# Squared norms of q in a hybrid S5 / gated-DeltaNet layer: turns of 32x32 squares, sums and a regrouping through DRAM in place of products with a column of ones

## The chip, the core and the metric

The kernel runs on one core of a Trainium2 chip. The metric is the device time of one execution in microseconds (us). The engines are PE (TensorE matmuls), PEld (TensorE weight loads, which overlap PE), DVE (VectorE), ACT (ScalarE), POOL (GpSimd) and SP (SyncE, which issues nearly all transfers here).

## What is computed

One residual layer on x of 1024 x 2048 in float32: a norm, one wide input projection, an S5 state-space branch, a gated DeltaNet branch of 8 heads x 128, a merge and an output projection. The change lies in the DeltaNet branch, where q and k of each head are divided by their lengths:

```python
def l2norm(t):
    return t * lax.rsqrt(jnp.sum(t * t, axis=-1, keepdims=True) + EPS)
...
q = l2norm(q.reshape(bsz, l, DN_HEADS, DN_HEAD_DIM))
k = l2norm(k.reshape(bsz, l, DN_HEADS, DN_HEAD_DIM))
...
o = gated_delta_rule(q, k, v, g, beta)
o = rmsnorm(o, norm_w) * jax.nn.silu(z)
```

Because o is linear in q and is normed itself afterwards, the kernel never divides q: the sum of squares of each q row goes into the small term of o's norm, at the end of the head.

## The kernel before

The sequence is worked in two passes of 512 tokens. In each pass PE goes through a plan of projection columns in stripes of 128 (`plan`): for each head its k, q, v and z stripes and two gate stripes, with the S5 input stripes `u` in between, then the S5 gate stripes, then the up projections and the output projection. A stripe is a sum over 16 (or 8) k-tiles, and each k-tile is three products of 128 x 128 by 128 x 512, since each operand is split into a high part and a low rest (`whi`, `wlo`). The weights come in halves of 512 KB (`raw`, three buffers, loaded on SP's queue); ACT copies a quarter-stripe chunk of them to `whi`, DVE subtracts to get `wlo`, and `w_next` keeps four chunks (`LA = 4`, four k-tiles each) ready ahead of PE.

All other work is written as Python generators in lanes (`epi`, `io`, `chain`, `prep`, `tab`, `s5`, `out`, `x`). After each k-tile `pump()` lets each lane take one step, if a planner (`Clock`, fed by the table `COST`) thinks that the step's inputs are there and that DVE is not too far behind PE. The planner's times only set the order in which instructions are written; each engine then works through its own list in that order, and waits where an input is not ready. `drain` writes out all that is left of a lane.

The lane `prep` holds `d_prep(h)`, one per head: ACT squares q into the tile `LU` (128 features x 512 tokens), PE turns k (`ident` products into bank 2), ACT squares the turned k with running sums, DVE writes `kd` (the row `M<-p,ex`), PE multiplies `LU` with a column of ones (bank 5, read by DVE into `nq_`), then k times k and k times q (`p<-M`, 128 x 256), a triangular solve with a trip through DRAM (`lu_d`, `tu_d`), all on slices of one tile block that the profile calls M. `d_chain(h)` follows with the state recurrence, and reads `nq_` at its end. Small per-token vectors lie in one tile, `smalls`.

The lane `s5` holds `s5_gen`: PE products into banks 6 and 7 (`p<-G0b`), then for two pairs a run of DVE work in the tile G0a (products with `p`, sums, two scans, products, and the sums into `sx`), then the output products `p<-G0a,G0b` of four `sx` pieces. In the first pass `s5_setup` runs ahead of it; its last stage is a loop of twelve 128 x 1024 DVE operations on the tile Y, and all that is left of it is drained when the plan comes to the first `u` stripe.

Where q's epilogue ends (`conv_epi`), DVE writes q into M by a SCALAR_TENSOR_TENSOR (`M<-tmp`), and all of the above for that head comes after it.

Of the kernel before, what the change touches and what calls it, by code (L numbers as in the profile page):

```python
# [11 lines left out]
F32 = mybir.dt.float32  # L12
# [4 lines left out]
AX = mybir.AxisListType  # L17
# [19 lines left out]
P = 128  # L37
# [56 lines left out]
class Timed:  # L94
# [3 lines left out]
    def __getattr__(self, name):  # L98
# [41 lines left out]
_VG = {"V": (0.07, 1.04e-3), "G": (0.14, 2.1e-3), "S": (0.05, 0.9e-3)}  # L140
_VF = {"V": (0.1, 0.6e-3), "G": (0.12, 1.1e-3), "S": (0.05, 0.9e-3)}
COST = {"tensor_tensor": _VG, "scalar_tensor_tensor": _VG, "tensor_scalar": _VF, "tensor_copy": _VF,
        "tensor_reduce": _VG, "activation": _VG, "tensor_tensor_scan": {"V": (0.07, 1.28e-3)},
        "memset": _VF, "reciprocal": {"V": (0.07, 8.3e-3)}, "iota": _VG, "matmul": None, "transpose": None, "dma_start": None}


@with_exitstack
def kernel(
# [27 lines left out]
    V = Timed(nc.vector, "V", clock)  # L176
    S = Timed(nc.scalar, "S", clock)
    G = Timed(nc.gpsimd, "G", clock)
    PE = Timed(nc.tensor, "PE", clock)
    SP = Timed(nc.sync, "Q", clock)  # L180
# [8 lines left out]
    dram = ctx.enter_context(tc.tile_pool(name="dram", bufs=1, space=bass.MemoryType.DRAM))  # L189
# [4 lines left out]
    def nm(s):  # L194
        uid[0] += 1
        return f"{s}_{uid[0]}"

    def bank(i):
        return psum.tile([P, 512], F32, tag=f"p{i}", name=nm(f"p{i}"))
# [7 lines left out]
    def small(tag, n, rows=P):  # L207
        if tag not in small_at:
            small_at[tag] = small_at.get("", 0)
            small_at[""] = small_at[tag] + n  # L210
        return smalls[0:rows, small_at[tag]:small_at[tag] + n]

    def tt(o, a, b, op, eng=None):
        (eng or V).tensor_tensor(o, a, b, op=op)

    def ts(o, a, s1, s2, op0, op1=None):
        if op1 is None:
            V.tensor_scalar(o, a, s1, None, op0=op0)
        else:
            V.tensor_scalar(o, a, s1, s2, op0=op0, op1=op1)  # L220
# [4 lines left out]
    MUL, ADD, SUB, MAX, MIN = ALU.mult, ALU.add, ALU.subtract, ALU.max, ALU.min  # L225
# [4 lines left out]
    ones = cpool.tile([P, P], F32, name="ones")  # L230
# [45 lines left out]

    lu_d = [dram.tile([4, 129, P], F32, name=f"lu_d{i}") for i in range(2)]
    tu_d = [[dram.tile([4, 129, P], F32, name=f"tu_d{i}{j}") for j in range(2)] for i in range(2)]
    st_d = dram.tile([8, P, P], F32, name="st_d")
    td_d = dram.tile([16, P, T], F32, name="td_d")  # L280
    ts_d = dram.tile([16, P, T], F32, name="ts_d")

    def part(d, off, *dims):

        a = d[:, :, :] if len(d.shape) == 3 else d[:, :, :, :]
        return bass.AP(tensor=a.tensor, offset=a.offset + off, ap=[list(x) for x in dims])
# [5 lines left out]
    def rows(d):  # L292
        return d[:, 0:P, :].rearrange("c s n -> s c n")
# [42 lines left out]
    def gts(o, a, s1, s2, op0, op1):  # L336
        G.tensor_scalar(o, a, s1, s2, op0=op0, op1=op1)
# [10 lines left out]
    for ps_ in range(NPASS):  # L348
# [8 lines left out]
        for c in range(8):  # L357
            if c % 2 == 0 and 8 - u0 + c // 2 < 8:
                i = 8 - u0 + c // 2
# [718 lines left out]
    def bc4(a):  # L1078
        return a.unsqueeze(2).broadcast_to([P, 4, P])
# [10 lines left out]
    def d_prep(h, ps_):  # L1090
        st = dw["set"][h % 2]
        kq, v, qk, U, kd = st["kq"], st["v"], st["qk"], st["U"], st["kd"]
        E, LU, mi = dw["E"], dw["LU"], dw["mi"]
        nk_, nq_, cc_ = nk[h % 2], nq[h % 2], cc[h % 2]
        lud, tud = lu_d[h % 2], tu_d[h % 2]
        pD = bank(5)
        for j in range(2):
            for i, gg in enumerate((gth, gtl)):
# [4 lines left out]
                          start=(i == 0), stop=(i == 1))  # L1103
# [9 lines left out]
            S.activation(mi[:, c, :], pK[:, c * P:(c + 1) * P], AF.Square, accum_out=nk_[:, c:c + 1])  # L1113
        tt(kd, pK.rearrange("p (c n) -> p c n", c=4), bc4(ex[:, 1, h * 4:(h + 1) * 4]), MUL)
        yield
        pQ = bank(5)
        for c in range(4):
            PE.matmul(pQ[:, c:c + 1], lhsT=LU[:, c, :], rhs=ones[:, 0:1], start=True, stop=True)

        rk = small("rk", 4)  # L1120
        gts(nk_, nk_, 1.0, 4e-6, MUL, ADD)
# [1 line left out]
        tt(cc_, cc_, bt[:, h, :], MUL, eng=G)  # L1123
        pow_small(rk, nk_, 4, "half")
        gts(rk, rk, 0.5, 1.0, MUL, MUL)
        ts(nq_, pQ[:, 0:4], 128e-6, 512e-12, MUL, ADD)
        yield
        for hf in range(2):
            pA = bank((5, 2)[hf])
            for c in (2 * hf, 2 * hf + 1):  # L1130
                PE.matmul(pA[:, (c % 2) * 256:(c % 2) * 256 + 256], lhsT=kq[:, c, 0, :],
                          rhs=kq[:, c].rearrange("p a n -> p (a n)"), start=True, stop=True)
# [2 lines left out]
            tt(qk[:, 2 * hf:2 * hf + 2, :], pa[:, :, 1, :], E[:, 2 * hf:2 * hf + 2, :], MUL)  # L1135
            yield
        tt(LU, LU, bc4(cc_), MUL)
        yield
        SP.dma_start(rows(lud), LU)
        yield  # L1140
# [11 lines left out]
        for j in range(15):  # L1152
            n = 15 - j
            a = ba[:, j, j + 1:16].unsqueeze(2).broadcast_to([32, n, j + 1])
            b = btm[:, j:j + 1, 0:j + 1].broadcast_to([32, n, j + 1])
# [33 lines left out]
        for b in B4:  # L1189
            for c in range(4):  # L1190
                PE.matmul(pU[b, c * 32:(c + 1) * 32], lhsT=g3[b, c, :], rhs=U[b, c, b], start=True, stop=True)
                PE.matmul(pU[b, P + c * 32:P + (c + 1) * 32], lhsT=U[b, c, b], rhs=g3[b, c, :],
                          start=True, stop=True)
# [8 lines left out]
        for o in (0, 64):  # L1202
            for c in range(4):
                PE.matmul(pg[o + 32:o + 64, c, 0:32], lhsT=LU[o:o + 32, c, o + 32:o + 64],
                          rhs=Tm[o:o + 32, c, o:o + 32], start=True, stop=True)
# [5 lines left out]
        for o in (0, 64):  # L1211
            for c in range(4):
                PE.matmul(pu[o:o + 32, c, 0:32], lhsT=gs[o + 32:o + 64, c, 0:32],
                          rhs=U[o + 32:o + 64, c, o + 32:o + 64], start=True, stop=True)
                PE.matmul(pu[o + 32:o + 64, c, 0:32], lhsT=U[o + 32:o + 64, c, o + 32:o + 64],
                          rhs=gs[o + 32:o + 64, c, 0:32], start=True, stop=True)
        for o in (0, 64):
            S.activation(U[o:o + 32, :, o + 32:o + 64], pu[o:o + 32, :, 0:32], AF.Copy, scale=-1.0)
        for o in (0, 64):
            S.activation(Tm[o + 32:o + 64, :, o:o + 32], pu[o + 32:o + 64, :, 0:32], AF.Copy, scale=-1.0)  # L1220
        yield

        pG = bank(5)
        pg = pG.rearrange("p (c n) -> p c n", c=4)
        for c in range(4):
            PE.matmul(pg[64:128, c, 0:64], lhsT=LU[0:64, c, 64:128], rhs=Tm[0:64, c, 0:64],
                      start=True, stop=True)
# [4 lines left out]
        for c in range(4):  # L1232
            PE.matmul(pu[0:64, c, 0:64], lhsT=gs[64:128, c, 0:64], rhs=U[64:128, c, 64:128],
                      start=True, stop=True)
# [140 lines left out]
    for ps_ in range(NPASS):  # L1375
# [49 lines left out]
        for kind, i, c0 in plan[ps_]:  # L1425
# [128 lines left out]
            elif kind in "qkv":  # L1554
                if kind == "k":
                    add("prep", i, d_prep(i, ps_))
# [126 lines left out]
```

## Time and profile before

| | |
|---|---|
| device time, median of three runs | 3029.99 us (3028.96 to 3030.83) |
| profiled execution, its own time | 3029.73 us |
| its span, first to last instruction | 3027.8 us |
| PE busy | 2974.2 us (98%) |
| DVE busy | 1662.4 us (55%) |
| ACT busy | 1152.2 us (38%) |
| mean granted TensorE clock | 0.993 of full speed |

All lines of the kernel pass through one recording helper, so every row has the line number L135, and groups are told apart by the names of their tiles, with buffer numbers left out. A float32 product is recorded as two matmuls with two weight loads. Time between the span and the device time (1.9 us) lies before the first and behind the last instruction.

### The profile page before, as it was taken

The page shows a single profiled execution, that of the slowest core. Times are in us where ns is not written, and L with a number is a line of the kernel's source. Part 1 is how long each engine was busy: PE and PEld are TensorE (multiplying, and loading weights), DVE is VectorE, ACT ScalarE, POOL GpSimd, SP SyncE. Part 2 cuts the span into 40 slices and gives each one's busy share as a digit, 9 for nine tenths or more (in the row PEclk, how much of TensorE's full clock was granted, in tenths as well). Part 3 has the DMA queues.
Part 4 walks back from the last instruction along what each step waited for, and adds up shares of the span by engine and source line. Part 5 has one row for each costly group of instructions (what it writes and reads, how often), then busy time and mean ns, then how long its engine had stood idle before and what let it go on. Part 6 is the DMA issues. An engine that isn't in the chain of part 4 may idle for free.

```text
span 3027.8 us, 42544 instructions
## 1 busy us (share of the span) xinstructions
PE 2974.2 (98%) x16030; PEld 2391.6 (79%) x16030; DVE 1662.4 (55%) x3082; ACT 1152.2 (38%) x2483; POOL 449.3 (15%) x857
## 2 busy tenths in 40 slices
PE   8989999999999999999999999999999999999998
PEld 6877777777777888888878777777777788888887
DVE  5746676777777522553454575567557633226542
ACT  5434544554454222334333333333433322223331
POOL 4412222122200000000033221222112000000000
PEclk9999999999999999999999999999999999999999
DMA  6525444444445644446354344444444464445541
GB/s 168 133 57 154 122 121 130 111 117 122 133 135 166 191 122 120 144 134 238 119 160 134 108 114 115 133 114 117 119 126 120 123 207 122 122 122 153 197 151 56
DMA packets 582143, 405.02 MB, mean 134 GB/s; under 512 B 55161, under 2 KB 515122, under 8 KB 580018
## 3 DMA queue, kind: packets, MB, share of 16 engines
q1 hardware_dynamic: 579634, 393.92, 45.3%
q0 software_dynamic: 2304, 8.39, 0.8%
q8 instruction: 126, 2.06, 0.3%
q14 instruction: 79, 0.65, 0.1%
HBM read 335.66 MB, written 66.58 MB: 133 GB/s over the span
## 4 chain that ended last, share of the span: by engine, by line
PE 85%; DVE 7%; POOL 2%; ACT 2%; issue 1%; DMA 1%; SPq 0%; DVEq 0%; POOLq 0%; ACTq 0%
PE p L135 85%; DVE G0a L135 2%; POOL M L135 2%; DVE M L135 2%; DVE wlo L135 1%; DVE tmp L135 1%; ACT M L135 1%; DMA raw<-in_w_in_dram 0%; DVE Y L135 0%; POOL smalls L135 0%; DMA M<-tu_d 0%; SPq L135 0%; ACT whi L135 0%; ACT L135 0%; ACT tmp L135 0%
## 5 line engine op out<-in xcount | busy, mean ns | idle before, releaser
L135 PE MATMUL p<-X,whi 128*128 128x512 f32 (+1 forms) x4432 | 1398.7, 398 | 1.9 <-DVE whi L135 0.8
L135 DVE TENSOR_TENSOR wlo<-raw,whi 128x512 fp32r<-128x512 f32 x920 | 631.0, 698 | 700.9 <-ACT whi L135 700.1
L135 PEld LDWEIGHTS p<-X,whi 128*128 128x128 f32 (+1 forms) x4432 | 802.8, 188 | 177.1 <-issue 19.9
L135 PE MATMUL p<-X,wlo 128*128 128x512 f32 (+1 forms) x2184 | 854.2, 391 | 8.0 <-DVE wlo L135 7.9
L135 ACT ACTIVATE whi<-raw 128x512 fp32r<-128x512 f32 x917 | 557.7, 625 | 512.6 <-PE p L135 485.0
L135 PE MATMUL p<-Y,whi 128*128 128x512 f32 (+1 forms) x1808 | 568.8, 396 | 1.9 <-ACT whi L135 1.1
L135 PEld LDWEIGHTS p<-X,wlo 128*128 128x128 f32 x2184 | 411.7, 189 | 97.6 <-DVE wlo L135 9.1
L135 PEld LDWEIGHTS p<-Y,whi 128*128 128x128 f32 (+1 forms) x1808 | 329.9, 187 | 72.8 <-ACT whi L135 2.6
L135 PE MATMUL p<-Y,wlo 128*128 128x512 f32 x896 | 349.8, 390 | 0.0
L135 POOL TENSOR_SCALAR smalls<-smalls 128x4 f32<-128x4 f32 (+1 forms) x58 | 15.7, 270 | 1603.8 <-DVE smalls L135 1109.4
L135 ACT ACTIVATE tmp<-p 128x512 f32<-128x512 f32 x160 | 95.5, 597 | 401.8 <-PE p L135 391.9
L135 POOL TENSOR_TENSOR M<-M 32x28 f32<-32x28 f32 (+8 forms) x492 | 190.7, 388 | 289.4 <-DMA M<-lu_d 194.2
L135 DVE TENSOR_TENSOR G0a<-G0a 128x256 f32<-128x256 f32 (+1 forms) x432 | 212.3, 528 | 3.4
L135 PEld LDWEIGHTS p<-M 32*32 32x32 f32 (+2 forms) x3072 | 153.5, 123 | 72.6 <-ACT M L135 32.7
L135 PEld LDWEIGHTS p<-Y,wlo 128*128 128x128 f32 x896 | 168.3, 188 | 36.5 <-DVE wlo L135 0.4
L135 PE MATMUL p<-M 32*32 32x32 f32 (+3 forms) x3072 | 187.2, 215 | 7.5 <-ACT M L135 3.8
L135 ACT ACTIVATE M<-p 32x128 f32<-32x128 f32 (+3 forms) x337 | 99.3, 298 | 159.9 <-PE p L135 156.2
L135 DVE SCALAR_TENSOR_TENSOR tmp<-tmp,vec 128x512 f32<-128x512 f32 x144 | 115.6, 803 | 11.9 <-ACT tmp L135 8.5
L135 DVE TENSOR_TENSOR_SCAN G0a<-rho,scar,G0a 128x256 f32<-128x256 f32 x128 | 89.7, 742 | 0.0
L135 DVE TENSOR_TENSOR G0a<-p,G0a 128x512 f32<-128x512 f32 x128 | 82.0, 682 | 13.4 <-PE p L135 10.8
L135 PE MATMUL p<-whi,G0a 128*128 128x512 f32 x280 | 88.5, 391 | 0.0
L135 PE MATMUL p<-whi,X 128*128 128x512 f32 x256 | 82.2, 393 | 0.0
(210 smaller groups left out, 2655.4 us busy)
## 6 DMA issues: line engine op xcount, KB each, us to landing
raw<-in_w_in_dram SPq DMA_DIRECT2D x324, 512.0 KB, 4.0
raw<-in_w_out_dram SPq DMA_DIRECT2D x56, 512.0 KB, 3.9
raw<-in_dn_w_up_dram SPq DMA_DIRECT2D x32, 512.0 KB, 4.1
raw<-in_s_w_up_dram SPq DMA_DIRECT2D x32, 512.0 KB, 3.8
td_d<-tmp SPq DMA_DIRECT2D x32, 256.0 KB, 2.0
M<-tu_d SPq DMA_DIRECT2D x32, 256.0 KB, 3.8
cs_d<-G0a SPq DMA_DIRECT2D x32, 256.0 KB, 2.3
yg_d<-G0a SPq DMA_DIRECT2D x64, 128.0 KB, 2.4
```

The source lines that it names most:

```text
L135: return f(*a, **k)
```

## The change

The four products with ones per head go, with their read-out by DVE. DVE instead turns each 32 x 32 square of the 128 x 512 tile `LU` (into the tile `U`, whose own use comes later) and sums each turned row of 32, which leaves 128 x 16 partial sums. These are written to a DRAM tile `nq_d` and read back by four transfers, so that the four partial sums of a token stand side by side in its partition: each transfer gathers 32 x 16 single floats. A last sum of four and the old scaling come later, in the solve. The planner's table gets a price for the turn, without which it couldn't place one.

```diff
-        "memset": _VF, ..., "transpose": None, "dma_start": None}
+        "memset": _VF, ..., "transpose": {"V": (0.07, 1.04e-3)}, "dma_start": None}
...
+    nq_d = [dram.tile([1, P, 16], F32, name=f"nq_d{i}") for i in range(2)]
...
+        qs_ = small(f"qs{h % 2}", 16)
...
-        pQ = bank(5)
-        for c in range(4):
-            PE.matmul(pQ[:, c:c + 1], lhsT=LU[:, c, :], rhs=ones[:, 0:1], start=True, stop=True)
+
+        LUf, qt = LU.rearrange("p c n -> p (c n)"), U.rearrange("p c n -> p (c n)")
+        V.transpose(qt, LUf)
+        V.tensor_reduce(qs_[:, 0:16], qt.rearrange("p (i n) -> p i n", n=32), op=ADD, axis=AX.X)
+        SP.dma_start(nq_d[h % 2][0], qs_[:, 0:16])
...
-        ts(nq_, pQ[:, 0:4], 128e-6, 512e-12, MUL, ADD)
         yield
...
         tt(LU, LU, bc4(cc_), MUL)
+
+        for j in range(4):
+            SP.dma_start(qs_[32 * j:32 * j + 32, :].rearrange("p (c b) -> p c b", c=4),
+                         part(nq_d[h % 2], j, (16, 32), (4, 4), (512, 4)))
         yield
         SP.dma_start(rows(lud), LU)
...
+        V.tensor_reduce(nq_, qs_.rearrange("p (c b) -> p c b", c=4), op=ADD, axis=AX.X)
+        ts(nq_, nq_, 128e-6, 512e-12, MUL, ADD)
 
         pG = bank(5)
```

As the planner's times change, so does the order of much else. Three places matter later. The first is PE's list in the second pass, head 4 (heads are counted from 0), at the S5 output products; X is the activations. Before:

```order
L135 MATMUL p_2144_16638<-X_1462_11596,whi_16619 128x512 x2
L135 MATMUL p_2144_16638<-X_1462_11596,wlo_16620 128x512
L135 MATMUL p_2144_16638<-X_1462_11596,whi_16639 128x512 x2
L135 MATMUL p_2144_16638<-X_1462_11596,wlo_16640 128x512
L135 MATMUL p_2156_16729<-ones,M_1700_13069 128x1 x4
L135 MATMUL p_2157_16740<-G0b_12917,G0a_12916 128x256
L135 MATMUL p_2157_16740<-G0a_12916,G0b_12917 64x256 x4
```

And with the change:

```order
L135 MATMUL p_2132_16678<-X_1454_11622,whi_16679 128x512 x2
L135 MATMUL p_2132_16678<-X_1454_11622,wlo_16680 128x512
L135 MATMUL p_2132_16678<-X_1454_11622,whi_16679 128x512 x2
L135 MATMUL p_2132_16678<-X_1454_11622,wlo_16680 128x512
L135 MATMUL p_2132_16678<-X_1454_11622,whi_16679 128x512 x2
L135 MATMUL p_2132_16678<-X_1454_11622,wlo_16680 128x512
L135 MATMUL p_2144_16781<-G0b_12943,G0a_12942 128x256
L135 MATMUL p_2144_16781<-G0a_12942,G0b_12943 64x256 x4
```

The products with ones are gone; between the turning of k and the S5 output products there are now five k-tiles where there were four.

The second place is DVE's list at the same point, from q's last epilogue step (`M<-tmp`) on. Before:

```order
L135 SCALAR_TENSOR_TENSOR M_1700_13069<-tmp 128x4x128
L135 TENSOR_TENSOR M_1700_13069<-p_2152_16695,ex 128x512
L135 TENSOR_TENSOR G0a_12916<-G0a_12916 128x256 x2
L135 COPY G0a_12916<-scar 128x2
L135 COPY scar<-G0a_12916 128x2
L135 TENSOR_TENSOR wlo_16723<-raw_16617,whi_16722 128x512
L135 TENSOR_SCALAR smalls<-p_2156_16729 128x4
```

And with the change:

```order
L135 SCALAR_TENSOR_TENSOR M_1692_13095<-tmp 128x4x128
L135 TENSOR_TENSOR M_1692_13095<-p_2140_16736,ex 128x512
L135 TENSOR_TENSOR G0a_12942<-G0a_12942 128x256 x2
L135 COPY G0a_12942<-scar 128x2
L135 COPY scar<-G0a_12942 128x2
L135 TENSOR_TENSOR wlo_16761<-raw_16653,whi_16760 128x512
L135 STREAM_TRANSPOSE M_1692_13095<-M_1692_13095 128x512
L135 TENSOR_REDUCE smalls<-M_1692_13095 128x16
```

The sums into `sx` (the row `G0a<-G0a 128x256 x2`) stand behind `kd` in both, and the turn and the sum come behind them.

The third place is DVE's list in the first pass, where the last stage of `s5_setup` runs on the tile Y. Before:

```order
L135 TENSOR_TENSOR wlo_2039<-raw_1736,whi_2038 128x512
L135 SCALAR_TENSOR_TENSOR G0b_174<-ident,G0b_174 128x128 x8
L135 TENSOR_TENSOR Y_2_146<-Y_2_146 128x1024 x2
L135 TENSOR_TENSOR Y_2_146<-Y_2_146 128x32x32
L135 TENSOR_TENSOR Y_2_146<-Y_2_146 128x1024 x2
L135 TENSOR_TENSOR Y_2_146<-Y_2_146 128x32x32
L135 TENSOR_TENSOR Y_2_146<-Y_2_146 128x1024 x2
L135 TENSOR_TENSOR Y_2_146<-Y_2_146 128x32x32
L135 TENSOR_TENSOR Y_2_146<-Y_2_146 128x1024 x2
L135 TENSOR_TENSOR Y_2_146<-Y_2_146 128x32x32
L135 SCALAR_TENSOR_TENSOR M_64_531<-p_233_2045,vec,M_64_531 128x512
L135 TENSOR_TENSOR wlo_2086<-raw_1736,whi_2085 128x512
```

And with the change:

```order
L135 TENSOR_TENSOR Y_2_148<-Y_2_148 128x1024 x2
L135 TENSOR_TENSOR Y_2_148<-Y_2_148 128x32x32
L135 SCALAR_TENSOR_TENSOR M_64_533<-p_231_2063,negc,M_64_533 128x128
L135 TENSOR_TENSOR M_64_533<-M_64_533,smalls 128x512
L135 TENSOR_TENSOR wlo_2079<-raw_1837,whi_2078 128x512
L135 TENSOR_TENSOR Y_2_148<-Y_2_148 128x1024 x2
L135 TENSOR_TENSOR Y_2_148<-Y_2_148 128x32x32
L135 TENSOR_TENSOR wlo_2098<-raw_1837,whi_2097 128x512
L135 SCALAR_TENSOR_TENSOR state<-state,ex,p_238_2110 128x128
L135 TENSOR_TENSOR M_64_533<-p_238_2110,M_64_533 128x128
L135 TENSOR_TENSOR wlo_2125<-raw_1983,whi_2124 128x512
L135 TENSOR_TENSOR Y_2_148<-Y_2_148 128x1024 x2
```

Before, the four rounds of the loop stand in one block, with no `wlo` between them; now one or more `wlo` stand between any two rounds.

## Rows read from the trace of the kernel before

**Rows 1.** The profile's page: busy time by engine; the chain that ended last.

```profile
PE 2974.2 (98%) x16030; PEld 2391.6 (79%) x16030; DVE 1662.4 (55%) x3082; ACT 1152.2 (38%) x2483; POOL 449.3 (15%) x857
...
PE 85%; DVE 7%; POOL 2%; ACT 2%; issue 1%; DMA 1%; SPq 0%; DVEq 0%; POOLq 0%; ACTq 0%
```

**Rows 2.** Groups by shape, PE and PEld: busy, mean ns, idle before, releaser.

```profile
L135 PE MATMUL p<-ones,M 128*128 128x1 f32 x128 | 16.2, 248 | 9.7 <-ACT M L135 9.7
...
L135 PEld LDWEIGHTS p<-ones,M 128*128 128x128 f32 x128 | 16.5, 195 | 13.1 <-ACT M L135 12.4
```

**Rows 3.** Timeline of PE, 108 to 112: start, length, what.

```profile
108.70 0.39 PE L135 MATMUL p<-X,wlo 128*128 128x512 f32 x1
108.92 0.95 PE L135 MATMUL p<-ones,M 128*128 128x1 f32 x8
...
110.29 0.40 PE L135 MATMUL p<-X,wlo 128*128 128x512 f32 x1
...
110.98 0.39 PE L135 MATMUL p<-X,wlo 128*128 128x512 f32 x1
```

**Rows 4.** Waits of PE, 1650 to 2350: total, times, longest.

```profile
PE p L135 <- ACT M L135: 10.1, 7, 1.7
```

**Rows 5.** Timeline of DVE, second pass, head 4, around q's epilogue.

```profile
1962.10 1.28 DVE L135 TENSOR_TENSOR G0a<-p,G0a 128x512 f32<-128x512 f32 x2
...
1984.02 0.69 DVE L135 SCALAR_TENSOR_TENSOR M<-tmp 128x512 f32<-128x512 f32 x1
1986.43 0.69 DVE L135 TENSOR_TENSOR M<-p,ex 128x512 f32<-128x512 f32 x1 [1.73 <-ACT M L135]
1987.04 0.75 DVE L135 TENSOR_TENSOR G0a<-G0a 128x256 f32<-128x256 f32 x2
...
1993.14 0.76 DVE L135 TENSOR_TENSOR M<-p,M 128x256 f32<-128x256 f32 x2 [4.32 <-PE p L135]
```

**Rows 6.** Timeline of PE at the same place.

```profile
1985.42 1.05 PE L135 MATMUL p<-ones,M 128*128 128x1 f32 x8 [1.73 <-ACT M L135]
...
1987.92 1.97 PE L135 MATMUL p<-G0a,G0b 128*64 128x256 f32 x6 [0.34 <-DVE G0a L135]
```

**Rows 7.** Windows: length, busy (instructions) of PE, PEld, DVE, ACT, POOL, clock, DMA share, GB/s.

```profile
217.00:235.00 18.00, 10.30 (x40) 8.13 (x39) 12.16 (x14) 1.12 (x2) 0.00 (x0) 0.81 0.48 157
1700.00:2300.00 600.00, 587.49 (x3549) 459.21 (x3548) 361.95 (x670) 224.44 (x560) 133.14 (x274) 0.98 0.44 119
...
1880.00:1892.00 12.00, 10.34 (x42) 7.22 (x42) 4.27 (x12) 4.56 (x16) 2.92 (x7) 0.72 0.24 66
1980.00:2000.00 20.00, 17.93 (x81) 12.86 (x80) 11.81 (x25) 6.23 (x19) 2.92 (x7) 0.91 0.19 51
```

**Rows 8.** Timelines of DVE and PE, 205 to 240, first pass.

```profile
211.00 14.71 DVE L135 TENSOR_TENSOR Y<-Y 128x1024 f32<-128x1024 f32 x12
...
227.03 0.80 PE L135 MATMUL p<-X,wlo 128*128 128x512 f32 x1 [7.70 <-DVE wlo L135]
...
230.60 0.39 PE L135 MATMUL p<-X,wlo 128*128 128x512 f32 x1
```

**Rows 9.** Groups by shape, DVE.

```profile
L135 DVE TENSOR_TENSOR_SCAN G0a<-rho,scar,G0a 128x256 f32<-128x256 f32 x128 | 89.7, 742 | 0.0
L135 DVE TENSOR_TENSOR G0a<-p,G0a 128x512 f32<-128x512 f32 x128 | 82.0, 682 | 13.4 <-PE p L135 10.8 <-DMA raw<-in_w_in_dram 2.6
...
L135 DVE TENSOR_SCALAR smalls<-p 128x4 f32<-128x4 f32 x16 | 2.5, 154 | 4.8 <-PE p L135 4.8
...
L135 DVE TENSOR_REDUCE smalls<-smalls 128x4 f32<-128x16 f32 x2 | 0.3, 170 | 0.0
```

**Rows 10.** SP's issues at 158 us, and transfers: KB each, us to landing.

```profile
158.63 3.27 SPq L135 DMA_DIRECT2D G0b<-in_s_d_dram  x4
...
raw<-in_w_in_dram SPq DMA_DIRECT2D x1, 512.0 KB, 5.0
G0b<-in_s_d_dram SPq DMA_DIRECT2D x4, 2.0 KB, 3.8
...
raw<-in_w_in_dram SPq DMA_DIRECT2D x324, 512.0 KB, 4.0
...
tu_d<-M SPq DMA_DIRECT2D x32, 32.0 KB, 1.8
```

More of the change, by code (lines that the diff above doesn't have):

```diff
@@ L143 @@
         "tensor_reduce": _VG, "activation": _VG, "tensor_tensor_scan": {"V": (0.07, 1.28e-3)},
-        "memset": _VF, "reciprocal": {"V": (0.07, 8.3e-3)}, "iota": _VG, "matmul": None, "transpose": None, "dma_start": None}
+        "memset": _VF, "reciprocal": {"V": (0.07, 8.3e-3)}, "iota": _VG, "matmul": None, "transpose": {"V": (0.07, 1.04e-3)}, "dma_start": None}
 @with_exitstack
```

## The prediction

> **What bounds the kernel now.** I read the page first: PE is busy 98% of the span, DVE 55%, and the chain that ended last is 85% PE and 7% DVE [rows 1]. So time is won where PE has less to do, waits less or gets a faster clock; work on DVE, ACT or SP counts only where PE comes to wait for it. The groups by shape give what is removed: 128 matmul records with ones (64 products, two records each) and as many weight loads, with 9.7 us of idle time right before them that ends with ACT's square of q [rows 2]. PE's waits in the second pass's head stretch show 10.1 us in seven waits for ACT [rows 4], nearly all of it in front of the ones of heads 2 to 7. The timelines at head 4 tell why: DVE is in one unbroken run of S5, weight and epilogue work from 1962.10 on, so that q's last epilogue step starts only at 1984.02 [rows 5]; ACT squares it, and PE, which was there 1.73 us before, starts its ones at 1985.42 [rows 6]. The windows show what follows such a pause: the granted clock, 1.00 elsewhere, is 0.91 over 1980 to 2000 and 0.72 over 1880 to 1892 [rows 7], so that PE runs at the lower of its two levels (1.2 in place of 2.4 GHz) for some microseconds. Over 1700 to 2300 the clock is 0.98, or 12 us of full-speed time lost. In the first pass one wait stands out: 7.70 us for `wlo`, since DVE works through twelve operations on Y in one block of 14.71 us [rows 8].
>
> **The products.** From the ordinary matmul at 108.70 to the next one of its kind behind the ones (110.29) PE takes 1.59 us; the same step without them (110.29 to 110.98) takes 0.69 [rows 3]. So four products with ones cost 0.90 us, less than the eight records' 248 ns each suggest, because they overlap. 16 heads x 0.90 = **14.4 us** off PE. The bounds are 13 (only the 0.81 us from their first start to the next matmul) and 16.2 (their busy time).
>
> **The wait in front of them.** It goes: 9.7 us. But DVE is as late as before, and the order shows which PE instruction is next to want it. In heads 4 to 7 these are the S5 output products: they need `sx`, and DVE has `sx` behind q's epilogue and behind `kd`, which itself waits for ACT's squares, so that it came at 1987.04 + 0.75 = 1987.8 [rows 5], and PE waited for it even behind the first wait [rows 6]. With the change PE meets these products one k-tile later than it met the ones (five instead of four behind the turn of k). It stood at the ones at 1985.42 - 1.73 = 1983.7; add 0.69 for the k-tile and 1.4 for six small products (the first output product, which needs no `sx`, and a chain step that the order now puts inside the stretch) at 0.69 / 3 each: 1985.8. `sx` at 1987.8 makes a wait of 2.0; the S5 input products that start DVE's run stand a k-tile earlier now, so DVE is a little less late, and I take 1.8. Four heads: 7.2. In heads 2 and 3 `sx` stands ahead of q's last step, three short DVE steps before it, and I take 0.7 each, 1.4. So **8.6 us of new waits for 9.7 old ones: 1.1** won. The bounds: none of it comes back (9.7 won), or each of the six is 1 us longer (5 lost).
>
> **The clock.** Of the 12 us I keep 1.8 in each of the four heads whose pause stays, as its length is that after which the clock fell at head 4 (0.09 of 20 us = 1.8), and let it go in the two with a short pause: **5 us** won; the bounds are 0 and 12.
>
> **The block on Y.** The new order puts `wlo` steps between its rounds. Twelve operations in 14.71 us make 3.7 us a round, and a chunk of weights lasts PE 4 x 0.69 = 2.8 us with four chunks ready ahead, so a round at a time does not run it dry. The 7.70 us go, and with them the slow matmuls up to 230.60: 3.57 us from 227.03 for three k-tiles of 0.69, or 1.5 us [rows 8], within the 0.81 clock of that window [rows 7]. Of 9.2 us I count **7**, as chain steps of head 0 now stand between the rounds and PE may wait for those; the bounds are 3 and 9.2.
>
> **DVE's new work.** No row shows a turn of squares, or a sum of 512 down to 16. The nearest are a product over 512 columns, 682 ns, above the sums of 16, 170 ns; a scan at 742 ns for 256 bounds each from above, at 1.5 us [rows 9]. I take 0.7 for each, as both walk 512 columns once, and 0.17 + 0.15 for the last sum and the scaling, less the read-out of 154 ns: 1.6 us a head net, 26 in all, between 0.5 and 3.2 a head. In the second pass the turn and the sum stand where DVE next idles 4.32 us for PE (up to 1993.14) [rows 5], so they are covered. In the first pass DVE is fuller, and I charge **2 us** in all, 0 to 8. If nothing covered them, 26 us would come back.
>
> The Trainium skill ("VectorE: DVE Perf Modes", "The three transpose paths") gives 311 ns for a 128x128 bf16 turn; four of them would be 1.24 us by estimate, 0.55 a head more than I take, which the same idle time covers. No row of this trace shows it.
>
> **The transfers.** Each head issues one store of 8 KB and four gathers of 512 single floats. The trace has four such gathers, of the same shape, at 158.63: SP needed 3.27 us to issue them, they landed in 3.8 us, and the one weight load beside them in 5.0 instead of 4.0 [rows 10]. The gathers wait on SP for the store (a small store lands in 1.8 us), and one weight load is queued behind them, so it goes up to 1.8 + 3.3 = 5.1 us late. A weight load is issued two halves, 4 x 2.8 = 11 us, ahead of ACT's copy, and takes 4.0 to 5.0: 6 us of slack, and four chunks more between ACT and PE. `lu_d`'s store, behind the gathers too, has DVE's two read-outs of k times q ahead of it anyway. **0 us**; without that cover some 5 us a head. The norms themselves are wanted only at the head's end.
>
> **The sum.** 14.4 + 1.1 + 5 + 7 - 2 = 25.5 us off the profiled execution's 3029.73, which stands 0.26 below the median of the runs: **3004**.
>
> **The rivals.** (A) The forecast. (B) No pause takes the place of the old one: PE finds `sx` ready, and the clock stays up: 14.4 + 9.7 + 12 + 9.2 = 45 us, 2984. For it speaks that PE's wait for G0a was only 0.34 before; against it, that DVE's run is as long. (C) The pause moves whole, each a little longer, the clock falls as before, and Y's gain is half: 14.4 - 4 + 0 + 4 = 14, 3015. (D) DVE's 26 us are not covered, above all in the first pass, and eat the rest: within 6 us of before. (E) Slower: the weight load behind the gathers comes later than its slack allows. A held-up load costs PE only beyond 6 + 11 us of delay; the delay is 5.1 as worked out above and grows with the gathers' landing, so it gets there when they land in 15.7 us in place of 3.8. From there each further us costs 16: at 17.3 the gain is eaten, at 18 the time is 3004 + 37 = 3041.
>
> For (E) speaks the Trainium skill, same page and section: a plain copy that turns data by strides is called 19 times slower than the turning transfer. The four gathers in this trace landed in 3.8 us each, so for 512 floats it doesn't bear this out.
>
> **Chances.** A 0.44, B 0.20, C 0.22, D 0.08, E 0.06. A, B and C are faster by over 0.2% (6 us, about what a measurement of this kernel can tell from no change): 0.86; D 0.08; E 0.06. Leaving out D, E and the far edge of B, the range is 2986 to 3021.
>
> **What would show it.** Right: no ones rows; PE's waits for ACT M down by about 10 us, and new ones for DVE G0a of some 9 us in the second pass; no wait of 7.7 us for `wlo` near 220; the clock of 1700 to 2300 at 0.99; STREAM_TRANSPOSE and the sum near 0.7 us; gathers that land in 3 to 5 us; no longer wait of ACT for `raw`. Wrong: waits for `raw` or `tu_d` that grow by over 10 us, PE waits in the first pass over 10 us more than before, or waits for G0a that are missing (B).

## The result, and the profile after

The changed kernel takes 2998.23 us (median of five runs, 2996.83 to 3000.75), against 3029.41 us (five runs, 3027.76 to 3030.83) for the kernel before. The ratio is 0.9897, with a 95% interval of 0.9884 to 0.9911: 31 us faster, well outside what a measurement can tell from no change. The profiled execution took 3000.75 us, its span 2998.7. Each trace below is of one execution; those of `old_order_no_norms`, `old_order_new_work` and `new_wait03` took 5 to 7 us more than the medians of their runs, so places are read from traces and the worth of a kernel from medians. The two lines of its page that answer to [rows 1], busy time and the chain that ended last:

```profile
PE 2952.0 (98%) x15902; PEld 2372.9 (79%) x15902; DVE 1676.4 (56%) x3130; ACT 1149.5 (38%) x2483; POOL 460.2 (15%) x857
...
PE 85%; DVE 6%; ACT 3%; POOL 2%; DMA 2%; issue 2%; SPq 1%; DVEq 0%; POOLq 0%; ACTq 0%
```

PE has 128 records less and is busy for 22.2 us less; the span is 29.1 us shorter. DVE has more to do than before. The new operations by shape (count, busy, mean ns), and then the transfers (KB each, median us to landing):

```profile
L135 DVE STREAM_TRANSPOSE M<-M 128x512 f32<-128x512 f32 x16 | 11.2, 701 | 0.0
L135 DVE TENSOR_REDUCE smalls<-M 128x16 f32<-128x512 f32 x16 | 11.0, 686 | 0.5
```

```profile
raw<-in_w_in_dram SPq DMA_DIRECT2D x324, 512.0 KB, 4.0
...
smalls<-nq_d SPq DMA_DIRECT2D x64, 2.0 KB, 3.2
```

Turn and sum take the 0.7 us each that the forecast gave them; the gathers land in 3.2 us and the weights in 4.0, as before. What PE waited for in the second pass (1650 to 2350; total, times, longest), which answers to [rows 4], and the windows that answer to [rows 7]:

```profile
PE p L135 <- DMA M<-tu_d: 3.8, 5, 0.8
PE p L135 <- DVE state L135: 2.3, 2, 1.8
PE p L135 <- DVE G0a L135: 1.7, 4, 0.4
PE p L135 <- POOL dhl L135: 1.6, 4, 0.4
PE p L135 <- ACT G0b L135: 1.2, 2, 0.7
PE p L135 <- ACT M L135: 0.7, 2, 0.5
```

```profile
217.00:235.00 18.00, 17.63 (x83) 14.34 (x82) 17.14 (x21) 6.01 (x13) 7.13 (x8) 1.00 0.57 138
1700.00:2300.00 600.00, 591.00 (x3582) 462.05 (x3582) 386.52 (x733) 230.25 (x572) 146.35 (x299) 1.00 0.46 122
```

The 10.1 us of waits for ACT M are down to 0.7, and the 8.6 us of new waits for DVE G0a that the forecast set against them are 1.7. The granted clock of 1700 to 2300 is 1.00 (before 0.98), and so is that of 217 to 235 (before 0.81): the block on Y no longer stops PE. Timelines of DVE, then PE, at head 4 of the second pass (start, length, what, the wait ahead of it), which answer to [rows 5, 6]:

```profile
1939.74 1.28 DVE L135 TENSOR_TENSOR G0a<-p,G0a 128x512 f32<-128x512 f32 x2
...
1963.37 0.68 DVE L135 SCALAR_TENSOR_TENSOR M<-tmp 128x512 f32<-128x512 f32 x1
1965.77 0.69 DVE L135 TENSOR_TENSOR M<-p,ex 128x512 f32<-128x512 f32 x1 [1.73 <-ACT M L135]
1966.38 0.75 DVE L135 TENSOR_TENSOR G0a<-G0a 128x256 f32<-128x256 f32 x2
...
1968.01 0.70 DVE L135 STREAM_TRANSPOSE M<-M 128x512 f32<-128x512 f32 x1
1968.74 0.69 DVE L135 TENSOR_REDUCE smalls<-M 128x16 f32<-128x512 f32 x1
...
1970.64 2.33 DVE L135 SCALAR_TENSOR_TENSOR tmp<-tmp,vec 128x512 f32<-128x512 f32 x3 [0.61 <-ACT tmp L135]
1973.57 0.76 DVE L135 TENSOR_TENSOR M<-p,M 128x256 f32<-128x256 f32 x2 [0.60 <-PE p L135]
```

```profile
1961.81 0.60 PE L135 MATMUL p<-ident,M 128*128 128x128 f32 x4
...
1966.22 0.65 PE L135 MATMUL p<-G0a,G0b 128*64 128x256 f32 x2
1967.27 1.08 PE L135 MATMUL p<-G0a,G0b 128*64 128x256 f32 x6 [0.40 <-DVE G0a L135]
```

The turn of k (`p<-ident,M`) is a fixed point of PE. Before, it stood at 1980.33 in PE's timeline of the same place. The S5 input products (`p<-G0b`), which DVE's run for S5 waits for, stood 28 k-tiles ahead of it and now stand 30; first the two lines before, then the one with the change:

```profile
1958.93 1.13 PE L135 MATMUL p<-G0b 64*128 64x256 f32 x8
...
1980.33 0.60 PE L135 MATMUL p<-ident,M 128*128 128x128 f32 x4
```

```profile
1936.95 1.14 PE L135 MATMUL p<-G0b 64*128 64x256 f32 x8
```

q's last epilogue step (`M<-tmp`) then began 3.7 us behind it (1984.02, [rows 5]); now it begins 1.6 us behind it (1963.37 less 1961.81). DVE's run for S5 begins 22.1 us ahead of it (1939.74), where it was 18.2 (1962.10). PE has 24.9 us of work between the S5 input products and the turn of k where it had 21.4: two k-tiles more, and small chain products that now stand there. DVE has no less to do (its run to the end of `sx` takes 27.4 us, before 25.7), but it starts earlier against PE, so `sx` is ready 5.3 us behind the turn of k in place of 7.5. So the question for the experiments was whether the work or the order of the lists had made the gain.

### The profile page after: what moved, and what is told of

Same layout as the page of the kernel before. It is cut to its first block, busy times and chain, and to the rows that moved or that the text cites. A ratio compares the mean times of both kernels' runs of the same rounds, so it can differ in the third digit from the quotient of the medians.

```text
span 2998.7 us, 42470 instructions
## 1 busy us (share of the span) xinstructions
PE 2952.0 (98%) x15902; PEld 2372.9 (79%) x15902; DVE 1676.4 (56%) x3130; ACT 1149.5 (38%) x2483; POOL 460.2 (15%) x857
## 4 chain that ended last, share of the span: by engine, by line
PE 85%; DVE 6%; ACT 3%; POOL 2%; DMA 2%; issue 2%; SPq 1%; DVEq 0%; POOLq 0%; ACTq 0%
PE p L135 85%; DVE G0a L135 2%; DVE M L135 2%; POOL M L135 2%; DVE wlo L135 1%; ACT M L135 1%; DVE tmp L135 1%; SPq L135 1%; POOL smalls L135 1%; DMA M<-tu_d 0%; ACT tmp L135 0%; ACT whi L135 0%; ACT L135 0%; ACT G0b L135 0%; DMA raw<-in_w_in_dram 0%
## 5 line engine op out<-in xcount | busy, mean ns | idle before, releaser
L135 PEld LDWEIGHTS p<-X,whi 128*128 128x128 f32 (+1 forms) x4432 | 802.0, 188 | 175.3 <-issue 17.9
L135 POOL TENSOR_SCALAR smalls<-smalls 128x4 f32<-128x4 f32 (+1 forms) x58 | 18.2, 313 | 1584.8 <-DVE smalls L135 1116.3
L135 POOL TENSOR_TENSOR M<-M 32x28 f32<-32x28 f32 (+8 forms) x492 | 196.7, 400 | 282.8 <-DMA M<-lu_d 200.1
```

The costliest lines, as they stand in the source:

```text
L135: return f(*a, **k)
```

## The experiments

### The order and the work taken apart

The planner can be charged for instructions that are not issued (`VP`, `SPP` and `PEP` below only move its times), and instructions can be issued that it is not charged for (`nc.vector`, ...). With that each way of taking the norms runs in either order; all other instructions stand in the lists exactly as in the kernel that gave the order.

New order, old products (`new_order_old_work`):

```diff
-        V.transpose(qt, LUf)
+        VP.transpose(qt, LUf)
...
+        pQ = bank(5)
+        for c in range(4):
+            nc.tensor.matmul(pQ[:, c:c + 1], lhsT=LU[:, c, :], rhs=ones[:, 0:1], start=True, stop=True)
...
+        nc.vector.tensor_scalar(nq_, pQ[:, 0:4], 128e-6, 512e-12, op0=MUL, op1=ADD)
```

> The order of every engine's list is that of the changed kernel, but the sums of squares are taken by the old products with ones, in the place of the turn. Theory 1 (the work decides; the order brings only the broken block on Y): 3029 - 9 = 3020, with some 10 us of PE's waits for ACT M in front of the ones of the second pass. Theory 2 (the order decides too: DVE comes to q's last epilogue step earlier against PE, so that nothing is waited for at this place): the changed kernel's 2998 plus 14.4 for the products = 3013, waits for ACT M in 1650 to 2350 under 3 us, clock there 1.00.

Old order, new work (`old_order_new_work`):

```diff
-            PE.matmul(pQ[:, c:c + 1], lhsT=LU[:, c, :], rhs=ones[:, 0:1], start=True, stop=True)
+            PEP.matmul(pQ[:, c:c + 1], lhsT=LU[:, c, :], rhs=ones[:, 0:1], start=True, stop=True)
+        nc.vector.transpose(qt, LUf)
...
+            nc.sync.dma_start(qs_[32 * j:32 * j + 32, :].rearrange("p (c b) -> p c b", c=4),
```

> The order is that of the kernel before, but the products with ones are gone and turn, sums and transfers stand in their place. Theory 1 (the work decides): 3029 - 14.4 - 9.7 and some of the clock = 3000 to 3005, PE's waits for ACT M gone and nothing of their size in their place; the wait of 7.7 us for wlo at 220 is still there. Theory 2 (in this order DVE is too late whatever PE does first): the pause moves to the S5 output products, as 2 to 3 us of waiting for DVE G0a in each of six heads, the clock of 1700 to 2300 stays at 0.98: 3029 - 14.4 and up to 5 more lost = 3015 to 3020.

Neither way, in the new order (`new_order_no_norms`) and in the old (`old_order_no_norms`, with `PEP` for the products): the sums of squares are left out, and a constant stands for them.

```diff
-        V.transpose(qt, LUf)
+        VP.transpose(qt, LUf)
...
+        nc.gpsimd.memset(nq[i], 512e-12)
```

> The changed kernel's order, with no sums of squares of q at all: turn, sums, store and gathers are left out and a constant stands for the norms of q. If DVE's new work and the transfers are covered (theory: 2 us in the first pass), 2996 to 2998. If DVE's 26 us count, 2972. If the gathers delay the transfers behind them so that PE's waits for tu_d grew by them (1.9 us before, 3.8 with the change), 2996 with those waits back at 1 to 2 us.

> The order of the kernel before, with no sums of squares of q at all: products and their read-out are left out and a constant stands for the norms of q. Theory 1 (the work decides): 3000 to 3005, as with the new work in this order. Theory 2 (the pause moves to the S5 output products): 3015 to 3018. The distance to the same order with the new work is what the turn, the sums and the transfers cost where no planner makes room for them: 0 to 3 us if DVE's idle time covers them, up to 26 if not.

Measured, medians in us (ratio to the kernel before, run beside them, with its interval):

| | products with ones | no norms at all | turn, sums, transfers |
|---|---|---|---|
| old order | 3030.4 (before) | 3017.8 (0.9952 to 0.9977) | 3027.7 (0.9982 to 1.0000) |
| new order | 3005.9 (0.9906 to 0.9933) | 2995.2 (0.9872 to 0.9899) | 2998.2 (the change) |

The new order alone, with the old products in it, gives 24.5 of the 31 us. The new work alone, in the old order, gives 2.7, which can hardly be told from nothing (its eleven runs lie from 3021.4 to 3033.0). The change itself was measured beside other runs of the kernel before, whose median was 1.0 us lower, so the steps to and from its cell are uncertain by about that. In both crossed runs the waits and the clock are those of theory 2, and the times went further than its figures (3005.9 for 3013, 3027.7 for 3015 to 3020). `old_order_no_norms` lies in theory 2's range, but the turn, sums and transfers cost 9.9 us in the old order, not 0 to 3. `new_order_no_norms` came out just under the 2996 to 2998 of covered work. Its waits of PE for `tu_d` in the second pass are 4.2 us, with the change 3.8, so the gathers did not bring that wait. PE's waits in the second pass of `old_order_new_work`, and then a window of it:

```profile
PE p L135 <- DVE G0a L135: 14.7, 6, 3.2
```

```profile
1700.00:2300.00 600.00, 583.07 (x3512) 456.84 (x3511) 371.58 (x691) 225.07 (x560) 131.86 (x273) 0.98 0.45 119
```

Six waits for ACT became six for `sx`, up to 3.2 us each, and the clock fell as before. `old_order_no_norms` has the same six waits; its DVE and PE at head 4 show how, without a turn in the way:

```profile
1957.29 1.28 DVE L135 TENSOR_TENSOR G0a<-p,G0a 128x512 f32<-128x512 f32 x2
...
1982.23 0.75 DVE L135 TENSOR_TENSOR G0a<-G0a 128x256 f32<-128x256 f32 x2
```

```profile
1975.53 0.60 PE L135 MATMUL p<-ident,M 128*128 128x128 f32 x4
...
1979.25 0.65 PE L135 MATMUL p<-G0a,G0b 128*64 128x256 f32 x2
1983.12 1.26 PE L135 MATMUL p<-G0a,G0b 128*64 128x256 f32 x6 [3.22 <-DVE G0a L135]
```

DVE needs from 1957.29 to 1982.98 for its run; PE, which has two of the eight products' records done at 1979.90, 4.4 us behind the turn of k, stands for 3.22 us. In the new order with the old products, the waits of the same stretch are:

```profile
PE p L135 <- DMA M<-tu_d: 4.1, 4, 1.1
PE p L135 <- POOL dhl L135: 1.5, 4, 0.4
PE p L135 <- DVE state L135: 1.4, 2, 0.8
PE p L135 <- ACT M L135: 0.8, 2, 0.5
```

The products with ones are there, and PE no longer waits for their square.

The trace of every kernel has the same 3064 ordinary `wlo` products, so times between the same two of them compare like with like (worked out from the PE timelines, us):

| | 384th to 896th (pass 1, products of 4 heads) | 1920th to 2256th (pass 2, products of 3 heads) |
|---|---|---|
| old order: products / none / new work | 460.5 / 456.6 / 456.6 | 308.1 / 308.2 / 308.0 |
| new order: products / none / new work | 457.6 / 453.5 / 453.8 | 300.1 / 300.3 / 299.7 |

In the stretch of the first pass PE's other waits differ by 0.2 us, and the products cost 3.9 and 4.1 us in four heads, 0.97 and 1.03 a head. In these heads of the second pass taking them away gains nothing in the traced executions of either order, because PE then arrives earlier at `sx` and waits.

What the order does in the second pass shows in the windows from the 1536th such product to the last, columns as in [rows 7]: before, the new order with the old products, and the change.

```profile
1552.11:2844.72 1292.61, 1276.78 (x6932) 1021.73 (x6931) 683.04 (x1220) 441.87 (x993) 212.98 (x394) 0.99 0.46 130
```

```profile
1545.72:2820.49 1274.77, 1265.35 (x6933) 1017.00 (x6932) 677.15 (x1220) 440.66 (x993) 219.45 (x394) 1.00 0.47 131
```

```profile
1542.88:2815.59 1272.71, 1260.11 (x6868) 1009.30 (x6867) 688.58 (x1244) 440.38 (x993) 217.83 (x394) 1.00 0.47 132
```

The first two have the same products. With the new order PE is busy with them for 11.4 us less, at a granted clock of 1.00 in place of 0.99, and idle for 6.4 us less: 17.8 in all. The change then takes another 5.2 us off PE's busy time, but 3.2 come back as idle time, so that leaving the products out wins 2.1 us here.

### The block on Y

One number of the planner breaks the block in the old kernel and closes it in the changed one. The lists of the second pass stay, but in the first pass other places move too, so neither run is of the block alone. `old_y_spread` and `new_y_whole`:

```diff
-SETUP = 2.0
+SETUP = 4.0
```

```diff
-SETUP = 2.0
+SETUP = 1.0
```

> The kernel before with one number of the planner changed (SETUP 4.0 in place of 2.0), which breaks the block of twelve operations on Y into 6, 3 and 3 with wlo between them; from there on the lists of the second pass stay as they were. Theory 1 (the block on Y is a part of the gain by itself, as the forecast has it: 7, bounds 3 to 9): 3030 - 7 = 3023, no wait of 7.7 us for wlo. Theory 2 (the wait only moves to the chain steps between the rounds): 3028 to 3030.

> The changed kernel with one number of the planner changed (SETUP 1.0 in place of 2.0), which puts the twelve operations on Y back into one block; the second pass stays as with the change. Theory 1 (the block costs the same here): 2998 + 7 = 3005, with a wait of some 7 us for wlo near 220. Theory 2: 2998 to 3000.

`old_y_spread` took 3023.9 us (0.9971 to 0.9988), 5.7 less than before and close to theory 1's 3023: the 7.70 us for `wlo` went, but the wait for Y below is new. It is not one between the rounds of the block. The longer part comes at 145.42, long before the block, where PE turns Y for an earlier stage of `s5_setup`. `new_y_whole` took 3018.1, some 20 more than the changed kernel. PE's waits from 100 to 300 in the one and the longest of them, then the waits over the whole span in the other, and its window:

```profile
PE p L135 <- DVE Y L135: 5.1, 2, 4.8
```

```profile
145.42 0.45 PE L135 MATMUL p<-ident,Y 128*128 128x128 f32 x1 [4.84 <-DVE Y L135]
```

```profile
PE p L135 <- DVE wlo L135: 9.9, 2, 9.7
...
PE p L135 <- ACT G0b L135: 7.3, 8, 1.0
PE p L135 <- DMA M<-tu_d: 6.0, 6, 1.2
```

```profile
217.00:235.00 18.00, 11.19 (x47) 8.86 (x46) 15.35 (x19) 4.18 (x9) 2.18 (x5) 0.78 0.17 58
```

Closing the block costs more there than its own wait: theory 1's sign held, its 7 us did not. Of the 17.6 us between the two traced spans, 11.0 lie between the 128th and the 384th `wlo` product, where the block stands, and 7.4 in the 512 behind them. There other things are late as well (ACT G0b 2.5 us with the change and 7.3 here over the span, `tu_d` 3.8 and 6.0), and the clock fell to 0.78 in the window. How much of this is the block and how much the other moves was not taken apart.

The two main kernels show the place itself. From the 178th to the 192nd `wlo` product PE has nothing but these 14 k-tiles, and they take 18.9 us before, 9.6 with the change, and 9.5 with the new order and the old products.

### Other orders

`new_wait03` and `new_price_measured` change one number of the changed kernel each:

```diff
-WAIT = 0.2
+WAIT = 0.3
```

```diff
-        ..., "transpose": {"V": (0.07, 1.04e-3)}, "dma_start": None}
+        ..., "transpose": {"V": (0.07, 1.23e-3)}, "dma_start": None}
```

> The changed kernel with another number of the planner changed (WAIT 0.3 in place of 0.2). In the second pass the S5 output products of the heads 3 to 6 now stand 29 k-tiles behind the S5 input products in place of 35. Theory 1 (that distance decides whether PE waits for DVE G0a): DVE's run, 27.4 us at head 4 of the changed kernel, meets 6 k-tiles or 4 us less of PE work, so waits for DVE G0a of 2 to 4 us a head come, and with them a lower clock: 3010 to 3025. Theory 2 (the second pass gains because the products are gone, not by this distance): 2995 to 3001.

> The changed kernel with the turn priced at what it takes by the trace (0.70 us for 512 columns, 1.23e-3 a column in place of 1.04e-3). The order changes in places, the S5 distance stays at 35 k-tiles and the block on Y is broken as with the change. If these two places of the order make the gain: 2995 to 3001. If the order decides in many small places by chance: further than 5 us from 2998.

`new_wait03` took 2997.5 us, not 3010 to 3025: the S5 distance alone does not decide. Its DVE, then its PE, at head 4:

```profile
1972.98 0.76 DVE L135 TENSOR_TENSOR G0a<-G0a 128x256 f32<-128x256 f32 x2
...
1974.54 0.69 DVE L135 SCALAR_TENSOR_TENSOR M<-tmp 128x512 f32<-128x512 f32 x1
1976.95 0.69 DVE L135 TENSOR_TENSOR M<-p,ex 128x512 f32<-128x512 f32 x1 [1.73 <-ACT M L135]
```

```profile
1972.23 0.60 PE L135 MATMUL p<-ident,M 128*128 128x128 f32 x4
...
1973.20 1.75 PE L135 MATMUL p<-G0a,G0b 128*64 128x256 f32 x8
```

Here `sx` stands ahead of q's last step in DVE's list, and ahead of `kd` with its 1.7 us of waiting for ACT, so it is nearly in time even 29 k-tiles behind. So what counts, by these rows, is the place of `sx` in DVE's list against the place of its reader in PE's. `new_price_measured` took 3003.8 us, 5.6 more than the changed kernel, above the range of the first theory and just past the 5 of the second: PE's waits for G0a in the second pass are 4.1 us, one of 2.5. Here a truer price made a worse order.

A version that beats both kernels follows: WAIT at 0.3 in the second pass alone (`new_pass2_wait03`), and its twin with the old products in the same order (`pass2_wait03_old_work`, edited like `new_order_old_work`).

```diff
-WAIT = 0.2
+WAIT = [0.2]
...
+        WAIT[0] = (0.2, 0.3)[ps_]
```

> The changed kernel, with the planner's WAIT at 0.3 in the second pass alone; the first pass keeps the order of the changed kernel. In the run with WAIT 0.3 throughout, the second pass took 7.0 us less than with the change, counted between the same k-tiles. Theory 1 (such a gain belongs to the order of the second pass alone): 2998 - 7 = 2991. Theory 2 (it hangs on the state in which the first pass leaves the lists): 2998 or more.

> The order of the run with WAIT 0.3 in the second pass alone, but the sums of squares by the old products with ones and their read-out, in the place of the turn. Theory 1 (the exchange of products for DVE's work is worth 7.7 us whatever the order, as between the two kernels that share the changed order): 7.7 above the run with the same order and the new work. Theory 2 (its worth depends on what else PE waits for there; 2.7 in the old order, 7.7 in the new): another figure, between 0 and 12.

They took 2991.2 us (0.9861 to 0.9886) and 3000.2 us (0.9890 to 0.9916). Theory 1 held for the first. In this order the exchange is worth 9.0 us, and three heads of the second pass take 293.9 against 296.7: 0.91 a head, the products' own price, since PE waits for neither ACT nor `sx` there. With 2.7, 7.7 and 9.0 in three orders, of which the last two can't be told apart (1.3 us, runs that spread over 3 to 6), the worth of the work depends on the order.

### How much cover is left

`new_turn_x3` and `new_gathers_x3`, in the new order:

```diff
+        nc.vector.transpose(qt, LUf)
+        nc.vector.tensor_reduce(qs_[:, 0:16], qt.rearrange("p (i n) -> p i n", n=32), op=ADD, axis=AX.X)
+        nc.vector.transpose(qt, LUf)
+        nc.vector.tensor_reduce(qs_[:, 0:16], qt.rearrange("p (i n) -> p i n", n=32), op=ADD, axis=AX.X)
```

```diff
+        for i in range(2):
+            for j in range(4):
+                nc.sync.dma_start(qx[i][32 * j:32 * j + 32, :].rearrange("p (c b) -> p c b", c=4),
...
```

> The changed kernel, its order kept, with the turn and the sum of 512 columns done three times over: 16 x 2 x 1.4 = 45 us more work on DVE. Theory 1 (the 3 us that the norms still cost in this order are DVE's, 2 of them forecast): 2998 + 2 x 3 = 3004. Theory 2 (they are the transfers'): 2998 to 3000. Were nothing covered: 3043.

> The changed kernel, its order kept, with the four gathers of every head issued three times (the second and third time into tiles that nobody reads): SP's queue is held 8 x 0.63 = 5 us longer in each head. Theory 1 (the forecast: the weight load behind them has 17 us of slack and is then some 10 us late): 2998 to 3000. Theory 2 (the 3 us that the norms still cost are the transfers', by loads of tu_d that come later): 2998 + 6 = 3004 or more, with PE's waits for tu_d above 6 us in all.

They took 3041.1 us (1.0031 to 1.0065; six runs from 3034.1 to 3051.7) and 3038.0 us (1.0020 to 1.0042), 43 and 40 more than the changed kernel. Both theories missed for the turns, which came near the figure for nothing covered. For the gathers theory 2 held by its signs, 3004 or more and `tu_d` above 6 us, though 40 us are far beyond the 6 that it starts from. The two longest totals among PE's waits over the whole span, of the turns and of the gathers:

```profile
PE p L135 <- DMA M<-tu_d: 16.5, 7, 3.0
PE p L135 <- DVE M L135: 15.6, 7, 5.2
```

```profile
PE p L135 <- DMA M<-tu_d: 16.9, 9, 5.2
PE p L135 <- DVE M L135: 6.9, 6, 3.9
```

The first turn and sum cost some 3 us, with the transfers; two more of each cost almost their whole 45. The head-4 rows of the changed kernel fit that: behind turn and sum DVE idles 0.61 and 0.60 us before the next step of the triangular solve, where 4.32 us stood before [rows 5]. The gathers hold up the solve's own trip through DRAM, which stands behind them on SP: PE's waits for `tu_d`, 3.8 us with the change, are 16.9, which is 13 of the 20 us by which all its recorded waits grow. The rest of the 35 us between the traced spans is busy time, at a mean clock of 0.991 in place of 0.996. That DVE's lateness also reaches PE through `tu_d` fits with the same chain (the solve's input is stored later), but only the waits show it.

## Why the prediction was right, and where it was not

3004 was forecast, 2998 measured, inside the range. The balance was about right; the account behind it was not, and that the sum came so near is partly luck.

- **Products, 14.4.** The price of 0.90 a head held roughly where PE's other waits are the same (0.91 to 1.03). But taking them away is worth 10.7 us in the new order (3005.9 to 2995.2) and 12.6 in the old, since in the second pass PE waits for `sx` in its place.
- **The wait in front of them, 1.1.** The mechanism, that the pause moves to `sx`, was right for the old order, more strongly than forecast (14.7 us in six waits). The failing step is "the S5 input products that start DVE's run stand a k-tile earlier now, so DVE is a little less late, and I take 1.8": they stand two k-tiles earlier, with chain products among them. The new order so gives DVE 3.8 us more ahead of the turn of k (22.07 against 18.23), and the waits were 1.7 us in all, not 8.6. The chain step that the forecast put between the turn of k and the output products is not there in the heads 4 to 7. The forecast had named missing waits for G0a as a sign of being wrong, and this sign came. The new order removes the wait even with the products left in, so it is not the missing products that removed it.
- **The clock, 5.** All of the 12 us of low clock in 1700 to 2300 are gone, as rival B had it, and no pause longer than 0.4 us came at those places. In the second pass the busy time of the same products falls by 11.4 us with the order, against the 5 of the forecast. How much of the 11.4 is the clock, and how much that products take longer just behind a pause, the rows do not separate.
- **The block on Y, 7.** At the place itself the whole 9.2 went (18.9 us to 9.6). Some of it was given back around it: from the 128th to the 384th `wlo` product the new order with the old products gains 4.5 us, with new waits for Y ahead of the block (1.7) and for a chain step's `state` behind it (1.6). So the term lay within its bounds of 3 to 9.2, and the chain steps, for which the forecast held some of it back, took their part. `old_y_spread`, with its 5.7, lies there too. Closing the block in the changed kernel, with what else that moves, costs 20, which no term foresaw.
- **DVE's new work, 2, and transfers, 0.** Together 3.0 us (2995.2 to 2998.2), most of it in the first pass (between the 128th and the 384th `wlo` product the profiled executions differ by 4.4, 260.0 against 255.5, more than the medians do in all). In the old order, which has no room for it, 9.9. The turn's 0.70 us agrees with the row that it was taken from [rows 9]. The Trainium skill ("VectorE: DVE Perf Modes", "The three transpose paths") led to an estimate of 1.24 us; the measurement decides against it. The same section of the Trainium skill warns of a copy 19 times slower where the innermost destination stride is large; the forecast left that condition out, and no run here uses the turning transfer that it compares with. The gathers land in 3.2 us, far from the 15.7 of rival E. The reason given for the transfers was wrong: the forecast looked for the 17 us of slack of the weight loads; what comes late first, at three times the gathers, is `tu_d`.

Of the 29.1 us between the two profiled executions, 11.1 lie in the first pass up to the 1536th `wlo` product, 19.9 in the second, and -1.8 ahead of the first. The forecast's terms come to 12.2 in the first pass (eight heads' products, Y, less 2) and 13.3 in the second, so it is the second pass that it had wrong. With the old products the new order alone gives 7.0 and 17.9 in the two passes. So the forecast took too much for the exchange of products for DVE's work (14.4 - 2, where 7.7 was measured) and too little for the order, which it read at single places and did not price as a whole; the two errors partly cancelled.

## What to carry to other kernels

Where a planner orders the lists by its own prices, a change of work is also a change of order, and the second can be the larger: run the new order with the old work, and the old order with the new, before saying what a change is worth. To see whether a wait goes or moves, compare how far the producer's run starts ahead of a fixed point of the consumer with how long the run is, in both orders. Work that was free the first time says nothing about the second: look at the idle time that is left behind it.

## What was not expected of the hardware

A short wait cost more here than its record. At head 4 of the changed kernel the eight S5 output products take from 1966.22 to 1968.35, 2.13 us, with a recorded wait of 0.40; in the new order with the old products the same eight run unbroken:

```profile
1971.15 1.23 PE L135 MATMUL p<-G0a,G0b 128*64 128x256 f32 x8
```

So a wait of 0.40 in the middle of the group took 0.90 us. The starts alone say the same: from the first of the eight to the k-tile behind them it is 2.06 us against 1.16. At head 5 the eight take 2.15 us with a wait of 0.43, and 1.21 without. That is as much as four products with ones cost, which fits with leaving those out having gained nothing in these heads.
